# The first two units of a decoder block take the input without its norm factor, which is multiplied onto their results, and the order of the opening is written out

## The chip, the cores and the metric

The kernel runs on one core of one Trainium2 chip. The core has a matrix engine (TensorE, PE in the profile; PEld are its weight loads), VectorE (DVE), ScalarE (ACT), GpSimd (POOL) and a sync engine (SP), which here issues all the transfers between memory (HBM) and the on-chip buffer (SBUF). TensorE writes its results to PSUM, eight banks of 128 x 512 words. Each engine works through its own list of instructions in order and waits on semaphores for the others. The metric is the device time of one execution in microseconds (us).

## The reference, cut to what matters

One decoder block with 2048 positions and 1024 features, all in 32-bit floats. What the change touches is the first norm and the first part of the input projection:

```python
def rmsnorm(x, g):
    y = x * lax.rsqrt(jnp.mean(x * x, axis=-1, keepdims=True) + 1e-6)
    return y * g
...
h = rmsnorm(x, norm1_g)                      # one factor for each position, one gain for each feature
proj = h @ w_in                              # 1024 -> 3088 columns
p_q, p_k, p_v, p_g, p_a, c_b, c_c, c_h = jnp.split(proj, splits, axis=-1)
gate_logits = p_a @ w_gate_up + b_gate       # p_a has 16 columns
log_a = jax.nn.log_sigmoid(gate_logits) / 16
o = rmsnorm(gla_chunked(q, k, v, log_a), gla_norm_g) * jax.nn.silu(p_g)
o_conv = c_b * causal_depthwise_conv(c_c * c_h, conv_w)
x = x + concatenate([o, o_conv]) @ w_out
x = x + (silu(rmsnorm(x) @ w_ffn_gate) * (rmsnorm(x) @ w_ffn_up)) @ w_ffn_down
return rmsnorm(x, norm_f_g)
```

The norm multiplies every position by a number of its own (the norm factor) and every feature by a gain. Since a product with `w_in` sums over features, the factor of a position may be multiplied before the product or after it; the gain may not.

## The kernel before, in words

Data lie by features: a tile holds 128 features by 512 positions. There are four blocks of 512 positions; blocks 0 and 1 form half 0, blocks 2 and 3 half 1. The input comes twice: `x` by rows of positions and `xt` by features.

*Products.* A 32-bit product is made of three products in a shorter format (`fp32r`): every operand is split into a high part, a copy by ScalarE (L163), and a low part, a subtraction by VectorE (L164); the products are high x high, high x low and low x high (L448 to L450). `wq` names split weights and `op` split inputs.

*Units.* The input projection has 12 units for each half. A unit takes 256 output columns, 1024 input features and the 1024 positions of the half, each side as 2 x 2 quarters. Units 0 and 1 of half 0 are computed plainly, with 96 products (L362 to L364, and L448 to L450 from `plain_unit`). All others use seven quarter products of 12 instead of eight, so 84 products: `unit_weights` (L424 to L441) has GpSimd make the sums S1 to S4 of weight quarters (L430, L431, L432, L437), and the inputs are B11, B21, B22 and the differences T1 to T4. In half 0 the differences are made by VectorE (L374), each 4 tiles. The results of a unit's products are put together by ScalarE copies (L480) and VectorE additions (L473).

*Opening.* `first_loads` loads the four row tiles of block 0 in halves, then the weights of unit 0, the rows of block 1 and block 1 by features. Each half row tile is squared and summed by ScalarE (L595) and turned by TensorE to the layout by features (L600, into PSUM). `rows_rstd` makes the norm factor from the sums: Ln and Exp on ScalarE, a refinement step on VectorE (last line L177), copies of the factor to 128 x 128 tiles (`rep`, L552), which TensorE transposes (L555, `rb_ps`) so that the factor stands along positions. `build_first` then multiplies input, gain and factor (L615), splits the result and issues unit 0's products; the factor of block 1 is made in their midst. The order of the work here comes from a scheduler, steered by marks: `tc.issue_after(m)` puts an instruction behind another in time, without a wait in the program where they are on one engine.

*Background.* `tick()`, called after each group of 12 products, advances a list of side tasks by one step: the weights of the gate, `pause(8)`, the gate of half 0 with its forget gates (`forget_gate`; Abs, Exp and Ln on ScalarE, scans on VectorE, last line L745) in turn with the sums of squares of blocks 2 and 3 (`row_stats`), then `h1_ahead`. That one loads half 1's input (L145), multiplies it with its factor, makes its differences on GpSimd, splits and stores the operands (L148, names beginning with `si`) until half 1 loads them. ScalarE changes its table of functions between Exp or Ln and Silu; each change is an ACT_TABLE_LOAD.

*After that.* Units 4 and 5 give the columns of `silu` (L512), units 6 to 11 those of the convolution, whose first line is L784 and second L786. Then follow the attention in chunks (as further background; products at L869), half 1's units, the output projection (L945) and the feed-forward part. Nothing of these is changed.

Of the kernel before, what the change touches and what calls it, by code (L numbers as in the profile page):

```python
# [52 lines left out]
def tile_hymba_block(ctx, tc, x, xt, win, wa, wgu, wout, wffn, wdown, wdown_first, small, out):  # L53
# [98 lines left out]
    second_weights, unit_splits, unsplit = [], [], []  # L152
# [8 lines left out]

    def split(src, hi, lo):
        last_hi[:] = [act.activation(hi, src, AF.Copy)]  # L163
        last_lo[:] = [dve.tensor_tensor(lo, src, hi.bitcast(F32), ALU.subtract)]  # L164
        return last_lo[0]
# [156 lines left out]
    def build_first(quad, w):  # L322


        ops = {b: [] for _, b in PRODUCTS}
        h, o = {}, {}
        quarters = ("A11", "A12"), ("A21", "A22")
        los = []

        def weight(n, i, *marks):  # L330
            with ExitStack() as stack:
                for m in (last_exp[0], *marks):
                    stack.enter_context(tc.issue_after(m.ins))
                w[n] = weight_quarter(first_raw[0][:, i, :])

        weight("A11", 0, last_copy[0])
        los.append(last_lo[0])
        for j in range(2):
            for r in range(2):
                o[r, j] = bank()  # L340
            for k in range(KD):
                with tc.issue_after(los[-2 if len(los) > 2 else -1].ins):
                    h[k, j] = quad(k, j)
                if (j, k) == (0, 0):
                    weight("A21", 3, last_scaled[0])
                x = opp.tile([P, 2, PB], F32R, name="op", tag="op")
                los.append(split(h[k, j][:], x[:, 0, :], x[:, 1, :]))
                hi = last_hi[0]
                if j == 0 and k in (1, 2):
                    weight(*(("A12", 1), ("A22", 2))[k - 1], los[-1])  # L350
                if j == 0 and k < PT:
                    with tc.issue_after(hi.ins):
                        row_squares(k)
                if (j, k) == (0, PT + 2):
                    rbs[1] = rows_rstd(squares[1][:, :, 0])
                name = ("B11", "B12")[j] if k < 4 else ("B21", "B22")[j]
                ops.setdefault(name, []).append(x)
# [206 lines left out]
    def row_squares(t):  # L564
        act.activation(rows[t], rows[t], AF.Square, accum_out=squares[1][:, t, 0:1])
# [822 lines left out]
```

## Time and profile before

| | |
|---|---|
| time, median of 3 runs | 2060.74 us (2060.27 to 2066.71) |
| span of the profiled execution | 2059.3 us |
| instructions in it | 27063 |
| granted clock of TensorE over the span | 0.996 of full |
| memory read, written | 274.98 MB, 144.70 MB |

The page gives no other time for the profiled execution than its span, from the first to the last instruction. Engines overlap, so their busy times add up to far more than the span. The page lists busy time by engine, the span in 40 slices, the chain of work that ended last, and the costliest groups of instructions. A group's row has line, engine, operation, `output<-inputs` and count, then busy time and mean, then idle time ahead of it and what ended most of it. A row in order of time has the start in us, the duration in us, engine, line and tiles; in brackets stands the wait ahead of it and what ended it. `fp32r` is the shorter format of the products.

### The profile page before, as it was taken

Reading aid. Unit: us, or ns where it says so; the run is one execution under the profiler, and the core shown is the slowest. Engines: PE = TensorE matmul, PEld = TensorE weight load, DVE = VectorE, ACT = ScalarE, POOL = GpSimd, SP = SyncE. Lnnn points to the kernel's source line nnn. Section 1 sums busy time; section 2 is a strip of 40 time slices with the busy share of each in tenths; the row PEclk is TensorE's granted clock in tenths of the full one; section 3 lists DMA queues with packets and bytes.
Section 4 is the critical chain, followed back from the end, with each engine's and each line's share of the span. In section 5 each row is a group of like instructions: output and inputs, shape, how many; then the busy total and the mean of one; then the engine's idle time right before and its main releaser. Section 6 shows DMA issues by size and latency. Waiting matters only on the chain.

```text
span 2059.3 us, 27063 instructions
## 1 busy us (share of the span) xinstructions
PE 2018.4 (98%) x9229; PEld 1657.3 (80%) x9229; DVE 1425.3 (69%) x2128; ACT 959.7 (47%) x1918; POOL 859.8 (42%) x622
## 2 busy tenths in 40 slices
PE   7999999999999999999999999999999999999997
PEld 6877888787888888888888878787888888878786
DVE  8789686559743886676675676767666666667774
ACT  6655365765542344444444452334434444453344
POOL 0345322122102564464564345534644544435544
PEclk9999999999999999999999999999999999999998
DMA  6378485416586873545454676476444434586653
GB/s 229 116 274 278 159 319 165 143 67 194 190 296 246 311 254 130 198 181 207 156 185 143 241 264 254 185 282 257 163 164 167 175 140 169 179 309 223 234 217 126
DMA packets 188729, 421.47 MB, mean 205 GB/s; under 512 B 19792, under 2 KB 65072, under 8 KB 178992
## 3 DMA queue, kind: packets, MB, share of 16 engines
q1 hardware_dynamic: 188592, 419.76, 57.2%
q8 instruction: 72, 1.18, 0.2%
q14 instruction: 65, 0.53, 0.1%
HBM read 274.98 MB, written 144.70 MB: 204 GB/s over the span
## 4 chain that ended last, share of the span: by engine, by line
PE 84%; DVE 7%; DMA 4%; ACT 3%; issue 1%; POOL 1%; SPq 0%; DVEq 0%; ACTq 0%; POOLq 0%
PE mm L448 24%; PE mm L449 23%; PE mm L450 23%; PE mm L945 3%; PE mm L948 3%; PE mm L946 3%; DVE wq L164 2%; DVE op L164 1%; DMA op<-sa_B 1%; DMA op<-sa_T 1%; PE a_ps L702 1%; ACT wq L163 1%; DMA siT<-lo 1%; PE o_ps L869 1%; PE o_ps L871 1%
## 5 line engine op out<-in xcount | busy, mean ns | idle before, releaser
L448 PE MATMUL mm<-op,wq 128*128 128x512 f32 x2499 | 973.7, 392 | 10.3 <-ACT c L480 5.3
L449 PE MATMUL mm<-op,wq 128*128 128x512 f32 x2499 | 972.5, 390 | 1.6 <-DVE op L164 1.6
L450 PE MATMUL mm<-op,wq 128*128 128x512 f32 x2499 | 961.3, 390 | 2.6 <-DVE wq L164 2.3
L164 DVE TENSOR_TENSOR wq<-raw,wq 128x512 fp32r<-128x512 f32 (+2 forms) x626 | 508.9, 818 | 262.6 <-ACT wq L163 260.0
L163 ACT ACTIVATE wq<-raw 128x512 fp32r<-128x512 f32 (+2 forms) x626 | 364.9, 589 | 585.6 <-PE mm L450 447.9
L448 PEld LDWEIGHTS mm<-op,wq 128*128 128x128 f32 x2499 | 468.9, 188 | 114.9 <-ACT c L480 8.0
L450 PEld LDWEIGHTS mm<-op,wq 128*128 128x128 f32 x2499 | 469.1, 188 | 103.8 <-DVE wq L164 6.1
L449 PEld LDWEIGHTS mm<-op,wq 128*128 128x128 f32 x2499 | 469.3, 188 | 99.1 <-DVE op L164 3.7
L432 POOL TENSOR_TENSOR raw<-s,raw 128x512 f32<-128x512 f32 (+2 forms) x97 | 133.3, 1374 | 518.5 <-DVE wq L164 474.7
L430 POOL TENSOR_TENSOR s<-raw 128x512 f32<-128x512 f32 (+2 forms) x97 | 127.4, 1313 | 247.5 <-DMA raw<-in_wffn_dram 90.7
L473 DVE TENSOR_TENSOR c<-mm,c 128x512 f32<-128x512 f32 x198 | 135.8, 686 | 72.7 <-PE mm L450 70.9
L473 DVE TENSOR_TENSOR y<-mm,y 128x512 f32<-128x512 f32 x185 | 126.9, 687 | 83.3 <-PE mm L450 82.9
L437 POOL TENSOR_TENSOR raw<-raw 128x512 f32<-128x512 f32 (+2 forms) x97 | 120.6, 1244 | 126.7 <-DVE wq L164 126.7
L927 POOL TENSOR_TENSOR ssx<-ssx,q 128x512 f32<-128x512 f32 x52 | 77.4, 1504 | 158.8 <-ACT q L926 158.5
L431 POOL TENSOR_TENSOR raw<-raw 128x512 f32<-128x512 f32 (+2 forms) x97 | 137.3, 1416 | 4.9
L480 ACT ACTIVATE c<-mm 128x512 f32<-128x512 f32 x198 | 116.1, 587 | 11.1 <-PE mm L450 9.3
L945 PE MATMUL mm<-op,wq 128*128 128x512 f32 x256 | 100.9, 395 | 0.0
L946 PE MATMUL mm<-op,wq 128*128 128x512 f32 x256 | 99.7, 389 | 0.0
L163 ACT ACTIVATE wq<-s 128x512 fp32r<-128x512 f32 (+2 forms) x97 | 56.9, 587 | 89.3 <-PE mm L450 85.4
L164 DVE TENSOR_TENSOR wq<-s,wq 128x512 fp32r<-128x512 f32 (+2 forms) x97 | 82.6, 852 | 2.8 <-ACT wq L163 2.1
L164 DVE TENSOR_TENSOR op<-op 128x512 fp32r<-128x512 f32 x94 | 76.8, 844 | 4.7 <-ACT op L163 4.6
L948 PE MATMUL mm<-op,wq 128*128 128x512 f32 x256 | 79.8, 390 | 0.0
(204 smaller groups left out, 1807.6 us busy)
## 6 DMA issues: line engine op xcount, KB each, us to landing
raw<-in_wffn_dram SPq DMA_DIRECT2D x44, 1024.0 KB, 6.5
sa_B<-so SPq DMA_DIRECT2D x47, 512.0 KB, 4.2
op<-sa_B SPq DMA_DIRECT2D x47, 512.0 KB, 7.1
raw<-in_win_dram SPq DMA_DIRECT2D x23, 1024.0 KB, 5.4
sa_T<-so SPq DMA_DIRECT2D x44, 512.0 KB, 4.5
op<-sa_T SPq DMA_DIRECT2D x44, 512.0 KB, 6.9
raw<-in_wdown_dram SPq DMA_DIRECT2D x24, 768.0 KB, 5.8
sx<-y SPq DMA_DIRECT2D x48, 256.0 KB, 4.0
```

Source lines behind the costliest of these rows:

```text
L163: last_hi[:] = [act.activation(hi, src, AF.Copy)]
L164: last_lo[:] = [dve.tensor_tensor(lo, src, hi.bitcast(F32), ALU.subtract)]
L430: pool.tensor_tensor(s1, a21, a22, ALU.add)
L431: pool.tensor_tensor(a21, a11, a21, ALU.subtract)
L432: pool.tensor_tensor(a11, s1, a11, ALU.subtract)
L448: pe.matmul(o[:], wh, xh, start=first and k == 0, stop=False, skip_group_check=True)
L449: pe.matmul(o[:], wh, xl, start=False, stop=False, skip_group_check=True)
L450: return pe.matmul(o[:], wl, xh, start=False, stop=k == n - 1, skip_group_check=True)
L473: dve.tensor_tensor(t[:], o[:], t[:], ALU.add)
L945: pe.matmul(o[e, j][:], wh, m[:, 0, :], start=k == 0, stop=False)
L946: pe.matmul(o[e, j][:], wh, m[:, 1, :], start=False, stop=False)
L948: pe.matmul(o[e, j][:], wl, ops[k][j][:, 0, :], start=False, stop=k == KD - 1)
```

## The change

- *Units 0 and 1 of half 0* take the input of blocks 0 and 1 by features (`xt`) with the gain but without the norm factor. The gain is applied in the split (`split_in_order`): as the scale of ScalarE's copy and as the scalar of VectorE's operation. The factor is multiplied onto the 8 result tiles by VectorE (`out`), in place of ScalarE's copies.
- *Units from 2 on* take normed inputs as before. These are made by `normed` (input x gain x factor, 16 of them), and B11, B21 and B22, which before were the operands of units 0 and 1, are split once more (`made`).
- *The rows* of blocks 0 and 1 are still loaded and squared, for the factor; they are no longer turned by TensorE. Twelve products of a tile of ones (`warm`) are issued ahead of everything.
- *The order.* `opening` gives the order of loads, and `queued` puts each instruction of ScalarE and VectorE behind the one issued before on its engine. The low half of a split is issued behind the next split's high half (`late`, `catch_up`). Transposes of the factor are put behind a product in TensorE's order (`turn`): the first behind the first three steps of unit 0's second column, the second behind the first 24 products of unit 1. The products after them are put behind the transposes.
- *Unit 2* has the making of the last operands and the outputs of unit 1 put between the splits of its weights (`between`).
- *Background.* Unit 1 no longer calls `tick`. The list begins with `pause(1)`, the gate's weights, `pause(5)`.
- `rows_rstd`, now for blocks 2 and 3 alone, is what it was for them.

```diff
+    tails, late, ordered = {}, [], []
+    def queued(eng, issue):
+        with behind([tails[eng]] if eng in tails else []):
+            tails[eng] = issue()
+        return tails[eng]
+    def catch_up():
+        while late:
+            last_lo[:] = [queued(dve, late.pop(0))]
+    def split_in_order(src, hi, lo, gain=None):
+        scale = 1.0 if gain is None else gain
+        last_hi[:] = [queued(act, lambda: act.activation(hi, src, AF.Copy, scale=scale))]
+        catch_up()
+        top = hi.bitcast(F32)
+        if gain is None:
+            late.append(lambda: dve.tensor_tensor(lo, src, top, ALU.subtract))
+        else:
+            late.append(
+                lambda: dve.scalar_tensor_tensor(lo, src, gain, top, ALU.mult, ALU.subtract)
+            )
...
         w["S1"] = weight_quarter(s1)
+        others()
         w["S2"] = weight_quarter(a11)
+        others()
...
+        warm = bank("warm")
+        for _ in range(12):
+            pe.matmul(warm[:, 0:P], ones[:], ones[:], start=True, stop=True)
+        fetch_w(0)
+        fetch_x(0, 0)
+        fetch_w(3)
+        for k in (1, 2, 3):
+            fetch_x(k, 0)
+        fetch_w(1)
+        fetch_x(4, 0)
+        fetch_w(2)
+        fetch_x(5, 0)
+        for t in (0, 1):
+            fetch_rows(0, t)
+        for k in (6, 7):
+            fetch_x(k, 0)
+        for t in (2, 3):
+            fetch_rows(0, t)
+        for k in range(KD):
+            fetch_x(k, 1)
+        raw = raw_weights(win[1])
+        for t in range(PT):
+            fetch_rows(1, t)
+        raw2 = raw_weights(win[2])
...
+        def turn(rep, mark):
+            rb = bank("rb_ps")
+            with behind([mark]):
+                for t in range(PT):
+                    done = pe.transpose(rb[:, t * P : (t + 1) * P], rep[:, t, :], ident[:])
+            return rb, done
...
+        def normed(k, j):
+            y = h[k, j][:]
+            queued(
+                dve,
+                lambda: dve.scalar_tensor_tensor(
+                    y, y, col(C_G1 + k), rbs[j][:], ALU.mult, ALU.mult
+                ),
+            )
+        def out(o, dst, j):
+            c = tt("c")
+            queued(dve, lambda: dve.tensor_tensor(c[:], o[:], rbs[j][:], ALU.mult))
+            store(dst[:], c[:])
...
+        for k in range(KD):
+            column(k, 0)
+        operand(0, 1)
+        est = first_estimate(0)
+        operand(1, 1)
+        operand(2, 1)
+        rep = spread(*est)
+        catch_up()
+        for k in range(3):
+            mark = column(k, 1)
+        rb, turned = turn(rep, mark)
+        operand(3, 1)
+        keep(0, rb)
...
+        catch_up()
+        with behind([turned]):
+            for k in range(3, KD):
+                column(k, 1)
+        normed(2, 0)
+        out(o[0, 0, 0], s_kq[0][0], 0)
+        normed(3, 0)
+        out(o[0, 1, 0], s_kq[0][1], 0)
+        for n, i in (("A11", 0), ("A21", 3)):
+            weight(n, raw[:, i, :])
+        made("B11")
+        square(1, 0)
+        square(1, 1)
+        for n, i in (("A12", 1), ("A22", 2)):
+            weight(n, raw[:, i, :])
+        square(1, 2)
+        square(1, 3)
+        for k in range(4, KD):
+            normed(k, 0)
+        est = first_estimate(1)
+        catch_up()
+        rep = spread(*est)
...
+        rb, turned = turn(rep, second(0, 0))
+        keep(1, rb)
+        with behind([turned]):
+            for j, i in ((0, 1), (1, 0), (1, 1)):
+                second(j, i)
+        for k in range(4):
+            normed(k, 1)
+        for r in range(2):
+            out(o[0, r, 1], s_kq[1][r], 1)
+        for k in range(4, KD):
+            normed(k, 1)
+        made("T1")
+        between = [
+            [partial(made, "T2")],
+            [partial(out, o[1, r, 0], s_kq[0][2 + r], 0) for r in range(2)],
+            [partial(made, "B21")],
+            [partial(out, o[1, r, 1], s_kq[1][2 + r], 1) for r in range(2)]
+            + [partial(made, "T3")],
+            [partial(made, "B22")],
+            [partial(made, "T4")],
+        ]
+        return ops, raw2, between
...
-            gate_weights(), pause(8), in_turn(gate(0, ops), row_stats(2), row_stats(3)),
+            pause(1), gate_weights(), pause(5), in_turn(gate(0, ops), row_stats(2), row_stats(3)),
```

More of the change, by code (lines that the diff above doesn't have):

```diff
@@ L1250, in tile_hymba_block @@
     act.preload_act_table_set("natural_log_exp_and_others")
[L1251 to L1254 removed]
+    ops, raw, between = opening()
     hurry.append(True)
```

328 lines of the change are left out of this document (166 added, 162 removed).

## The prediction, made before the changed kernel had run

> **What bounds the kernel now.** I read the page first, then stretches of the span, then the order of time on single engines.
>
> ```profile
> span 2059.3 us, 27063 instructions
> PE 2018.4 (98%) x9229; PEld 1657.3 (80%) x9229; DVE 1425.3 (69%) x2128; ACT 959.7 (47%) x1918; POOL 859.8 (42%) x622
> PE   7999999999999999999999999999999999999997
> PE 84%; DVE 7%; DMA 4%; ACT 3%; issue 1%; POOL 1%; SPq 0%; DVEq 0%; ACTq 0%; POOLq 0%
> ```
>
> TensorE carries the chain; only the first and the last slice of 51 us show much idle time. The change touches the opening, so what counts is how late TensorE stands when unit 2, 3 and the later units of half 0 begin.
>
> ```profile
> core 0: us, PE busy (x) PEld busy (x) DVE busy (x) ACT busy (x) POOL busy (x), PEclk, DMA share, GB/s
> 0.00:16.39 16.39, 6.63 (x37) 5.77 (x37) 7.53 (x23) 10.47 (x26) 1.11 (x7) 1.00 0.84 294
> 16.39:63.82 47.43, 45.95 (x196) 37.61 (x197) 44.18 (x79) 27.86 (x54) 12.54 (x4) 0.96 0.48 176
> 63.82:83.10 19.28, 19.28 (x85) 15.76 (x84) 9.63 (x13) 10.46 (x22) 3.43 (x3) 1.00 0.27 95
> 120.00:145.00 25.00, 25.00 (x113) 20.61 (x112) 19.27 (x40) 14.23 (x25) 11.30 (x9) 1.00 0.73 250
> 145.00:200.00 55.00, 51.72 (x224) 41.50 (x223) 50.09 (x57) 25.84 (x49) 36.24 (x24) 1.00 0.89 305
> 10.00:20.00 10.00, 5.59 (x25) 4.33 (x24) 8.14 (x20) 8.35 (x21) 0.00 (x0) 0.83 1.04 403
> ```
>
> Rows are stretches (start:end, length), then busy time and count by engine. Units 0 and 1 (192 products of 512 columns, and 4 transposes) run from 16.39 to 63.82, unit 2 (84) to 83.10. In unit 2 TensorE issues 85 instructions in 19.28 us, 0.227 each, which is its full pace. So before 16.39 the time is lost, and VectorE is the next engine: 44.18 busy of 47.43, with slack only in unit 2 (9.63 of 19.28).
>
> ```profile
> 2.18 5.07 DMA xr<-in_x_dram
> 4.96 0.63 ACT L595 ACTIVATE q<-xr 128x512 f32<-128x512 f32 x1 [2.89 <-DMA xr<-in_x_dram]
> 16.39 0.73 PE L362 MATMUL mm<-op,wq 128*128 128x512 f32 x1 [2.42 <-ACT op L163]
> 19.90 0.39 PE L362 MATMUL mm<-op,wq 128*128 128x512 f32 x1
> 27.95 0.64 PE L555 MATMUL rb_ps<-ident,rep 128*128 128x128 f32 x4 [1.48 <-DVE rep L552]
> ```
>
> The first load is used at 4.96; the first product starts at 16.39, after transposes, norm factor and scaling. Up to 19.90 it runs at half clock (8 products in 3.51 us instead of 1.8: 1.7 lost), and block 1's factor costs 1.48 waited and 0.64 of transposes. With 1.7 and 2.1 lost, 192 x 0.227 = 43.6 becomes 47.4.
>
> **The change, step by step.**
>
> *Step 1, the start.* Gone: 32 transposes, 4 copies out of PSUM, the factor ahead of everything. The first product needs the second load of 256 KB (0.65 us each at 403 GB/s), so 4.96 + 0.65, and ScalarE's copy with a gain.
>
> ```profile
> L784 ACT ACTIVATE c<-u,sml 128x512 f32<-128x512 f32 x8 | 5.7, 718 | 4.1 <-DVE u L780 4.1
> 276.50 0.89 PE o_ps L869 x8
> ```
>
> The copy with a column as scale took 0.72, so the first product is at about 6.4. The 12 added warm-up products are plain fp32 (two records each): 0.11 a record as in the o_ps row, 0.22 a product, 0.44 at half clock, 5.3 us from 1.1 on, done at 6.4 as well. I take 6.5: **-9.9**. Whether the clock is full by then (0 or 1.7 lost) matters little, since the splits set the pace of the first products.
>
> *Step 2, the rest of units 0 and 1.* Loads are in the order of use, with 8 in flight. Counted in 256 KB, block 0's x(6) is the 15th (lands at 5 + 14 x 0.65 = 14), block 1's x(0) the 21st (18) behind four row tiles that ScalarE squares first. TensorE would want them at 15.5 and 18.7; with ScalarE's copies queued between, I count 3.0 us of waits on data in all, and 1.2 for the first weights of unit 1, whose low halves stand behind four products of the factor on VectorE. The larger wait is the second factor: its transposes stand in TensorE's order after 120 products, and 72 products are held behind them. They wait for VectorE, whose order is now given. Its built order up to the last `rep` holds 24 scalar_tensor_tensor, 14 tensor_tensor, 8 small operations and 8 copies.
>
> ```profile
> 28.63 1.41 DVE L615 SCALAR_TENSOR_TENSOR h<-h,sml,rb_ps 128x512 f32<-128x512 f32 x2 [0.42 <-PE rb_ps L555]
> 41.09 4.90 DVE L374 TENSOR_TENSOR h<-h 128x512 f32<-128x512 f32 x8
> 12.95 0.63 DVE L552 COPY rep<-msq 128x128 f32<-128x128 f32 x4
> 12.75 0.16 DVE L177 SCALAR_TENSOR_TENSOR msq<-rl,ry 128x4 f32<-128x4 f32 x1
> ```
>
> Back to back these are 0.66, 0.60, 0.18 and 0.2 apart: 15.8 + 8.4 + 1.6 + 1.4 = 27.2, from 5.5 on 32.7. It idles about 8 us on data and on ScalarE (3 for x(6), 2.7 for the squares and block 1's x(0), 1.6 for a copy that stands behind the factor's evacuation, the rest in short waits), and two GpSimd operations on unit 2's weights hold it 1.3 each (next rows). So `rep` is ready near 43.3. TensorE comes there at 6.5 + 120 x 0.227 + 3.0 + 1.2 + 0.5 = 38.4: a wait of 4.9. Unit 1 ends at 6.5 + 43.6 + 3.0 + 1.2 + 4.9 + 1.0 (two sets of transposes) = 60.2 against 63.82: **-3.6**.
>
> *Step 3, unit 2.* Twelve operands that were reused (B11, B21, B22) are now split anew from normed values: 12 more operations on each of ScalarE and VectorE; 16 normings replace 16 scalings; 8 results are multiplied by the factor on VectorE where ScalarE copied them.
>
> ```profile
> 54.12 8.83 POOL L432 TENSOR_TENSOR raw<-s,raw 128x512 f32<-128x512 f32 x1 [20.35 <-DVE wq L164]
> 61.12 0.69 DVE L374 TENSOR_TENSOR h<-h 128x512 f32<-128x512 f32 x1
> 62.99 0.64 ACT L163 ACTIVATE wq<-raw 128x512 fp32r<-128x512 f32 x1 [3.76 <-POOL raw L432]
> 106.33 1.63 POOL L432 TENSOR_TENSOR raw<-s,raw 128x512 f32<-128x512 f32 x1 [10.13 <-DVE wq L164]
> 106.70 1.28 DVE L216 TENSOR_TENSOR rl<-msq,ry 128x4 f32<-128x4 f32 x1
> ```
>
> VectorE and GpSimd exclude each other here: the GpSimd subtraction started at 54.12 ended only after VectorE's dense stream did (61.81, then 1.1 us), and at 106.70 a 0.16 us operation took 1.28 behind one. From `rep` to the last low half of T4 VectorE's order holds 8 scalar_tensor_tensor and 60 tensor_tensor: 5.3 + 36.0 = 41.3, from 44.6 (the factor is copied first) to 85.9; three GpSimd operations in the way at 1.3 and the copies' latencies add 4.6: 90.5. The first product on that operand is the 298th: without waits at 60.2 + 105 x 0.227 = 84.1. So **+6.4**, which leaves +2.8 at unit 3. Ends: 0, if VectorE keeps up, and 9, if the exclusion strikes each of the seven weights.
>
> *Step 4, the table loads.* The background list starts with unit 2 instead of unit 1: 8 calls fewer ahead of it and 2 less of pause, so 6 groups of 12 products, 16.3 us, later. The forget gates' Exp and Ln then fall beside unit 4's Silu.
>
> ```profile
> 111.90 0.21 ACT L745 ACTIVATE el<-g 128x4 f32<-128x4 f32 x1
> 120.88 1.28 ACT L512 ACT_TABLE_LOAD   x1
> 122.17 0.63 ACT L512 ACTIVATE c<-c 128x512 f32<-128x512 f32 x1
> ```
>
> Before, the last of them ended 9 us ahead of the first Silu. The built order holds 20 table loads against 15, the five extra ones around units 4 and 5: 5 x 1.28 = 6.4 us on an ACT that is busy 14.23 of 25 there. That share, 0.57, gives **+3.7**; ends 0 and 6.4. The Trainium skill (ScalarE: Activation LUTs, What ACT_TABLE_LOAD costs) gives 1283 ns and a drain of 1380 ns to every switch; the trace agrees with the first and shows 1.29 from the load to the next activation. By that page's 2.66 us the five would be 13.3, an estimate.
>
> *Step 5, what comes late after that.* Half 1's operands are made ahead in one chain of loads, VectorE, GpSimd and stores:
>
> ```profile
> 123.68 1.61 SPq L145 DMA_DIRECT2D h<-in_xt_dram  x3
> 188.11 1.78 DVE L786 SCALAR_TENSOR_TENSOR c<-u,sml,c 128x512 f32<-128x512 f32 x1
> 192.04 0.38 SPq L148 DMA_DIRECT2D siT<-t  x1
> ```
>
> It ran from 123.68 to 192.04, and TensorE lost 55.0 - 224 x 0.227 = 4.2 us from 145 to 200. It reached only 4 us into the convolution (first row of L786); some 20 us later it lies beside it and the loads of the attention stage, on a VectorE that was at 50.09 of 55 already. I take the loss once more: **+4.2**; ends 0 (it merely moves) and 8.4 (three times). The order from there on is the old one, and nothing gives time back.
>
> Sum: -3.6 + 6.4 + 3.7 + 4.2 = +10.7. That is 2070.0 against the profiled execution's 2059.3, which stands 1.4 under the median shown, so **2071 us**.
>
> **Rivals.**
> - *VectorE keeps up* (faster). If idle time on data in the opening goes and the factor is ready by 38.4, step 2 gives -8.5; it decides if T4 is then split by 79 instead of 90. The 8 us of idling speak for it, the sum of 27.2 + 41.3 against it: even dense it ends at 74 plus five holds of 1.3, 80. With steps 4 and 5 hidden: 2052.
> - *The later units absorb it.* ACT has room in 120 to 145, and the chain of step 5 has its own slack: only steps 1 to 3 count, +2.8: 2063.5. For it speaks TensorE's full 25.00 there.
> - *The switches cost more.* With the drain as a full stop of ACT on the path (5 x 2.66 for 3.7) and step 5 at its upper end: 2059.3 + 2.8 + 13.3 + 4.2 + 1.4 = 2081. The 1.29 speaks against it. By the page this is what would happen.
>
> **How the numbers follow.** 0.3% is 6.2 us, about what a measurement here can tell from none: 2054.6 to 2066.9 counts as the same. My forecast gets 0.57, VectorE keeping up 0.08, absorption 0.24, costly switches 0.11. The forecast's lower edge reaches into "same" rarely and absorption's upper edge out of it as often, so faster 0.08, same 0.24, slower 0.68. The range leaves out the faster case and the top of the costly one: 2061 (steps 4 and 5 nearly free) to 2080 (their upper ends, 6.4 and 8.4, are 2078).
>
> **What would show it.** Step 1: first product at 6 to 7 us. Step 2: a wait of TensorE on `rep` near 38, 3 to 7 us long. Step 3: TensorE waits on low halves of op in unit 2, between 62 and 92, 6 us in all, VectorE busy over 90% from 20 to 90. Step 4: 20 table loads, five of them within 120 to 145, and waits of TensorE on ACT there. Step 5: the last siT store near 215 and over 6 us lost between 145 and 225; from 300 on the same distance to the trace of before. The prediction is wrong if unit 2 ends before 80, or if the distance shrinks after 145.

## The result and the profile after

The changed kernel takes 2087.8 us (median of 4 runs, 2084.6 to 2088.6) against 2061.2: 26.6 us or 1.21% slower, ratio 1.0121 with a 95% interval of 1.0106 to 1.0135. The forecast was 2071 us. The direction came out as said, the size did not: by the end of half 0's convolution the trace is 24.75 us behind, where the prediction's sum was 10.7.

The page of the changed kernel: its first lines, VectorE's row of the 40 slices, and the chain.

```profile
span 2082.9 us, 27063 instructions
...
PE 2029.3 (97%) x9221; PEld 1658.5 (80%) x9221; DVE 1436.8 (69%) x2143; ACT 968.0 (46%) x1920; POOL 853.6 (41%) x622
...
DVE  7877777558764596766776577775775676677774
...
PE 80%; DVE 9%; DMA 5%; ACT 3%; issue 2%; POOL 0%; SPq 0%; DVEq 0%; ACTq 0%; POOLq 0%
```

The profiled execution is the fastest of the four (2084.6); its span is 23.6 us longer than before. VectorE's share of the chain rose from 7 to 9%, TensorE's fell from 84 to 80%.

To place the loss, count the long products of the units (512 columns, into `mm`) in the order in which they ran, and compare the start of the nth in both traces; the nth is here the one that has n ahead of it. The distance, after minus before, is -9.5 us at the first, -1.6 at the 192nd (end of unit 1), +10.0 at the 360th (as many as units 0 to 3 have; of the gate's 36 products the old kernel has done all by then and the changed one all but one), +17.6 at the 556th, and +24.75 from the 840th to beyond the 1000th. Below, stretches of the changed kernel cut at these products (start:end, length, then busy time and count by engine):

```profile
core 0: us, PE busy (x) PEld busy (x) DVE busy (x) ACT busy (x) POOL busy (x), PEclk, DMA share, GB/s
0.00:6.90 6.90, 5.49 (x25) 5.20 (x25) 2.33 (x8) 2.63 (x3) 1.11 (x7) 1.00 0.59 162
6.90:62.19 55.29, 48.61 (x201) 38.08 (x201) 45.59 (x76) 31.33 (x56) 7.29 (x5) 0.94 0.62 232
62.19:120.42 58.23, 51.74 (x205) 38.31 (x204) 43.52 (x65) 30.38 (x62) 11.14 (x8) 0.97 0.31 107
120.42:175.51 55.09, 47.32 (x206) 37.50 (x205) 42.69 (x97) 40.33 (x81) 19.76 (x14) 1.00 0.65 224
175.51:249.67 74.16, 67.55 (x282) 53.01 (x280) 61.63 (x81) 35.23 (x68) 36.86 (x25) 0.98 0.78 264
```

Before, the same stretches took 16.39, 47.43, 46.59, 47.48 and 67.03 us. So the start gained 9.5, and the four after it lost 7.9, 11.6, 7.6 and 7.1. The prediction had -9.9, then +6.3, +6.4, +3.7 and +4.2: every loss is there, and every one is too small.

Rows in order of time show the forecast wait on the second factor, and two of the waits in unit 2:

```profile
43.24 1.09 PE L630 MATMUL rb_ps<-ident,rep 128*128 128x128 f32 x4 [4.50 <-DVE rep L620]
...
69.62 0.50 PE L410 MATMUL mm<-op,wq 128*128 128x512 f32 x1 [1.59 <-DVE op L182]
...
95.91 0.50 PE L410 MATMUL mm<-op,wq 128*128 128x512 f32 x1 [1.33 <-DVE op L182]
```

What the prediction did not have is in the granted clock (column PEclk), shown here in stretches of 3.41 us, the steps in which it changed:

```profile
core 0: us, PE busy (x) PEld busy (x) DVE busy (x) ACT busy (x) POOL busy (x), PEclk, DMA share, GB/s
34.15:37.56 3.41, 3.41 (x17) 2.79 (x16) 3.41 (x6) 3.41 (x7) 0.53 (x1) 1.00 0.85 289
37.56:40.97 3.41, 1.18 (x6) 0.64 (x4) 3.41 (x4) 0.49 (x2) 2.84 (x2) 1.00 0.02 9
40.97:44.38 3.41, 1.14 (x5) 1.18 (x6) 2.42 (x11) 0.43 (x3) 0.00 (x0) 0.50 0.22 43
44.38:47.79 3.41, 3.41 (x9) 2.64 (x9) 2.80 (x5) 0.58 (x1) 0.00 (x0) 0.50 0.75 303
47.79:51.20 3.41, 3.41 (x16) 2.81 (x16) 3.41 (x6) 0.00 (x0) 0.00 (x0) 1.00 0.41 154
...
68.27:71.69 3.42, 1.34 (x5) 0.82 (x6) 3.42 (x5) 2.24 (x5) 1.67 (x1) 1.00 0.71 230
71.69:75.10 3.41, 3.41 (x10) 2.63 (x9) 3.41 (x7) 0.00 (x0) 0.00 (x0) 0.50 0.17 64
```

After a stretch in which TensorE was idle most of the time, the next is at half clock: 9 or 10 instructions in 3.41 us instead of 16. The wait of 4.5 us thus cost about 2.3 us more behind it (4.5 us of products at half speed), the waits around 70 about 1.7 (3.4 us at half speed); a third such stretch follows at 180.9.

### The profile page after: what moved, and what is told of

The parts are those of the page before. It is cut to its first block, busy times and chain, and to the rows that moved or that the text cites. A ratio compares the mean times of both kernels' runs of the same rounds, so it can differ in the third digit from the quotient of the medians.

```text
span 2082.9 us, 27063 instructions
## 1 busy us (share of the span) xinstructions
PE 2029.3 (97%) x9221; PEld 1658.5 (80%) x9221; DVE 1436.8 (69%) x2143; ACT 968.0 (46%) x1920; POOL 853.6 (41%) x622
## 4 chain that ended last, share of the span: by engine, by line
PE 80%; DVE 9%; DMA 5%; ACT 3%; issue 2%; POOL 0%; SPq 0%; DVEq 0%; ACTq 0%; POOLq 0%
PE mm L409 23%; PE mm L411 23%; PE mm L410 23%; PE mm L1093 2%; PE mm L1096 2%; PE mm L1094 2%; DVE wq L192 2%; DVE op L192 1%; DMA h<-in_xt_dram 1%; PE a_ps L856 1%; DMA ee<-sd 1%; ACT wq L191 1%; DVE op L182 1%; PE o_ps L1017 1%; PE o_ps L1019 1%
## 5 line engine op out<-in xcount | busy, mean ns | idle before, releaser
L409 PE MATMUL mm<-op,wq 128*128 128x512 f32 x2467 | 963.1, 393 | 17.6 <-ACT c L444 9.7
L410 PE MATMUL mm<-op,wq 128*128 128x512 f32 x2467 | 961.9, 390 | 6.0 <-DVE op L182 5.7
L411 PE MATMUL mm<-op,wq 128*128 128x512 f32 x2467 | 950.5, 391 | 5.0 <-DVE wq L192 4.9
L192 DVE TENSOR_TENSOR wq<-raw,wq 128x512 fp32r<-128x512 f32 (+2 forms) x612 | 494.8, 813 | 258.2 <-ACT wq L191 255.5
L191 ACT ACTIVATE wq<-raw 128x512 fp32r<-128x512 f32 (+2 forms) x612 | 355.6, 587 | 577.1 <-PE mm L411 440.3
L409 PEld LDWEIGHTS mm<-op,wq 128*128 128x128 f32 x2467 | 463.9, 188 | 123.8 <-ACT c L444 13.0
L411 PEld LDWEIGHTS mm<-op,wq 128*128 128x128 f32 x2467 | 463.7, 188 | 106.4 <-DVE wq L192 10.1
L410 PEld LDWEIGHTS mm<-op,wq 128*128 128x128 f32 x2467 | 464.0, 188 | 105.3 <-DVE op L182 9.7
L387 POOL TENSOR_TENSOR raw<-s,raw 128x512 f32<-128x512 f32 (+2 forms) x97 | 125.2, 1290 | 526.8 <-DVE wq L192 459.4
L1093 PE MATMUL mm<-op,wq 128*128 128x512 f32 x256 | 100.9, 395 | 0.0
L1094 PE MATMUL mm<-op,wq 128*128 128x512 f32 x256 | 99.7, 390 | 0.0
L1096 PE MATMUL mm<-op,wq 128*128 128x512 f32 x256 | 79.8, 390 | 0.0
```

Of the source, the lines that this page charges most:

```text
L387: pool.tensor_tensor(a11, s1, a11, ALU.subtract)
L409: pe.matmul(o[:], wh, xh, start=first and k == 0, stop=False, skip_group_check=True)
L410: pe.matmul(o[:], wh, xl, start=False, stop=False, skip_group_check=True)
L411: return pe.matmul(o[:], wl, xh, start=False, stop=k == n - 1, skip_group_check=True)
L1093: pe.matmul(o[e, j][:], wh, m[:, 0, :], start=k == 0, stop=False)
L1094: pe.matmul(o[e, j][:], wh, m[:, 1, :], start=False, stop=False)
```

## The experiments

Each kernel was run 4 to 11 times beside the old one on the same chip (the old one's median 2061.7 to 2062.9). "Faster" and "slower than the changed one" compare medians with its 2087.8; the interval of each ratio is 2 to 3 us to either side, so smaller differences between two runs are not shown by their times. Distances at the nth product are to the trace of the old kernel, as above.

### Is it the opening, or the background that it pushed back?

First run: the old kernel, with the background alone as late as in the changed one.

```diff
-            gate_weights(), pause(8), in_turn(gate(0, ops), row_stats(2), row_stats(3)),
+            gate_weights(), pause(14), in_turn(gate(0, ops), row_stats(2), row_stats(3)),
```

> The old kernel with its old opening, and only the background put where the changed kernel has it (6 product groups later; 20 table loads instead of 15). Theory A: the 14.8 us that the changed kernel loses between its 360th and its 840th product come from the late background alone; then this kernel is slower than before by 12 to 16 us, with the same distance of about 15 by the 840th product. Rival B: the background costs what the prediction priced (3.7 + 4.2 = 7.9), the rest comes from the opening, which leaves VectorE and ScalarE behind: slower by 6 to 9. Rival C: it is hidden when the opening is the old one: within 3 us.

Measured: 2073.7, ratio 1.0050 (1.0035 to 1.0064), so 11.4 us slower, and a distance of +0.2 at the 360th product and +12.7 at the 840th. That is just under A's 12 and far above the prediction's 7.9: of the 14.75 us that the changed kernel lost there, 12.5 come with the late background on the old opening too.

Second: the changed kernel with the background early.

```diff
-            pause(1), gate_weights(), pause(5), in_turn(gate(0, ops), row_stats(2), row_stats(3)),
+            gate_weights(), in_turn(gate(0, ops), row_stats(2), row_stats(3)),
```

> The changed kernel with both pauses of the background taken out, so that the gate's products stand after 264 of the long products instead of 300 and the program has 15 table loads. Theory A: the part after the 360th product falls from 14.8 us to 2 or less, and the kernel comes to 2070 to 2075; some of the gain is paid back in unit 2 and 3, where VectorE is full. Rival B: the loss stays above 6 us, as it is the opening's: 2078 to 2081. Rival C: the earlier background strikes the full VectorE in unit 2 and 3 and loses there what it saves: 2084 to 2088.

Measured: 2080.2, ratio 1.0088 (1.0072 to 1.0103). From the 360th to the 840th product only 1.5 us are lost, as A says. But at the 360th the distance is +16.2 instead of +10.0: between 61 and 115 us TensorE waits 6.4 us for high and low halves of unit 2's last operands, and runs at half clock for 10.2 and for 3.4 us. Both A and C are in it: 13.3 us saved late, 6.2 paid early. The time lies in B's range, but not by B's mechanism.

Fifth: the gate's steps first, the sums of squares after them, so that the forget gates end before the first Silu.

```diff
-            pause(1), gate_weights(), pause(5), in_turn(gate(0, ops), row_stats(2), row_stats(3)),
+            pause(1), gate_weights(), pause(4), gate(0, ops), row_stats(2), row_stats(3),
```

> The changed kernel with the second pause at 4 and the gate's steps ahead of the sums of squares instead of in turn with them: the forget gates end before the first Silu, the program has 15 table loads instead of 20, and the making of half 1's operands begins as late as before this edit. Theory (the table loads are the rise of 7.4 us between the 360th and the 500th product): this rise falls to 2 or less, the later one (7.2 us from the 556th to the 836th) stays, and the kernel is 5 to 7 us faster than the changed one: 2080 to 2083. Rival (the rise is ScalarE's whole load there, squares and splits, and not the loads of tables): within 2 us of it.

Measured: 2089.4, ratio 1.0127 (1.0112 to 1.0143): not faster. The rise went as the theory said: from the 360th to the 556th product 1.9 us instead of 7.6. But the distance at the 360th is +17.3, 7.3 more, probably since the gate's work now falls beside the operands of units 2 and 3 (not tested by itself), and the later rise is 9 instead of 7.1. So 5.8 us go with the five loads; the gate's own activations left the stretch with them, so that is their price together, while the squares of blocks 2 and 3 stayed there, so they alone don't make the loss. Moving the gate alone only moves the loss.

In the changed kernel, ScalarE's table loads in order of time:

```profile
132.93 1.28 ACT L476 ACT_TABLE_LOAD   x1
134.87 1.28 ACT L890 ACT_TABLE_LOAD   x1
140.88 1.28 ACT L897 ACT_TABLE_LOAD   x1
143.01 1.28 ACT L476 ACT_TABLE_LOAD   x1
145.57 1.28 ACT L899 ACT_TABLE_LOAD   x1
148.84 1.28 ACT L476 ACT_TABLE_LOAD   x1
```

and the stretch around them, from 120 to 145, where ScalarE was busy 14.23 us before:

```profile
core 0: us, PE busy (x) PEld busy (x) DVE busy (x) ACT busy (x) POOL busy (x), PEclk, DMA share, GB/s
120.00:145.00 25.00, 22.34 (x97) 17.84 (x96) 22.29 (x56) 23.14 (x51) 5.72 (x4) 1.00 0.65 230
```

Six where one stood, on a ScalarE that is now full: the squares of blocks 2 and 3 crowd there as well.

Sixth: the old kernel with only the making of half 1's operands late.

```diff
-            unhurried(),
+            pause(6), unhurried(),
```

> The old kernel with six more steps of pause between the sums of squares and the making of half 1's operands: forget gates and table loads (15) where they were, only that chain 6 product groups later. Theory (the chain beside the convolution costs by itself): slower than before by 5 to 8 us, the rise lying behind the 550th product. By the prediction's price it would be 4.2. Rival (it merely moves): within 2 us, and the 12.7 us of the first run were the table loads and what they delay.

Measured: 2069.7, ratio 1.0032 (1.0020 to 1.0045), slower by 7.3 us between the medians and by 6.6 by the ratio; the trace has +5.2 at the 840th product, all of it behind the 600th. The chain costs by itself when it is late.

Thirteenth: the same, with the chain's 16 differences on VectorE instead of GpSimd.

```diff
-    def combine(src, g, rb, put):
+    def combine(src, g, rb, put, eng=pool):
...
-            pool.tensor_tensor(t1[:], b12[:], b11[:], ALU.subtract)
+            eng.tensor_tensor(t1[:], b12[:], b11[:], ALU.subtract)
...
-        yield from combine(lambda k, j: xt[2 + j, :, k, :], C_G1, (rbs[2], rbs[3]), put)
+        yield from combine(lambda k, j: xt[2 + j, :, k, :], C_G1, (rbs[2], rbs[3]), put, dve)
...
```

> The sixth run (old kernel, half 1's operands made six product groups later, 6.6 us slower) with the 16 differences of that chain made by VectorE instead of GpSimd. Theory (what the late chain costs is GpSimd's holds on VectorE beside the convolution, as in unit 2): most of the 5.2 us that the trace lost there goes, 0 to 3 us slower than the old kernel. Rival (loads and the copies in ScalarE's queue set it, not GpSimd): 5 to 8 us slower as before this edit.

Measured: 2060.2, ratio 0.9996 (0.9987 to 1.0005): the 6.6 us are gone. The groups of VectorE between 157 and 230 us show what changed there. The sixth run (count, busy time, mean ns of one):

```profile
L164 DVE TENSOR_TENSOR lo<-t,hi 128x512 fp32r<-128x512 f32 x6 | 6.1, 1024 | 3.5 <-ACT hi L163 3.5
L164 DVE TENSOR_TENSOR lo<-h,hi 128x512 fp32r<-128x512 f32 x5 | 5.7, 1131 | 0.0
```

and the thirteenth:

```profile
L164 DVE TENSOR_TENSOR lo<-t,hi 128x512 fp32r<-128x512 f32 x6 | 4.1, 680 | 0.0
L164 DVE TENSOR_TENSOR lo<-h,hi 128x512 fp32r<-128x512 f32 x5 | 3.4, 681 | 0.0
```

Without GpSimd's differences the chain's own low halves take 0.68 us each instead of 1.02 and 1.13. The chain itself is shorter too: its last store of `siT` starts at 198.8 us instead of 204.1. How much each of the two is worth was not separated.

Fourteenth: this edit with the chain at its old time.

> The old kernel with the same edit alone (chain at its old time). Between 145 and 200 us TensorE lost 4.2 us. Theory: GpSimd's holds are part of that, 1 to 4 us faster than the old kernel. Rival: the same within 1 us.

Measured: 2063.7, ratio 1.0013 (1.0004 to 1.0022): no gain, 2 us slower if anything, which neither the theory nor the rival had. The trace is 5.4 us behind at the 800th product, most of it lost in one wait of 2.7 us on a ScalarE copy that ends at 203.5 us and a stretch of 6.8 us at half clock around it. That a chain without GpSimd is faster at any time is not shown; that it is no longer dear when late is.

### What bounds unit 2?

Third: the second factor's transposes behind 48 products of unit 1.

```diff
-        rb, turned = turn(rep, second(0, 0))
+        second(0, 0)
+        rb, turned = turn(rep, second(0, 1))
...
-            for j, i in ((0, 1), (1, 0), (1, 1)):
+            for j, i in ((1, 0), (1, 1)):
```

> The changed kernel with the transposes of the second factor put behind 48 products of unit 1 instead of 24, so that TensorE has 5.4 us of work while it waited 4.5 us for the factor (and ran at half clock for 6.8 us after). Theory (VectorE sets the pace to the end of unit 2): unit 1 ends about 6 us earlier, and nearly all of it goes back in unit 2, where the operands T2 to T4 come no earlier: the end changes by less than 2 us. Rival: the wait stands on the path: 5 to 7 us faster than the changed kernel, 2078 to 2082.

Measured: 2084.5, ratio 1.0104 (1.0089 to 1.0119), 3.3 us faster than the changed one. The trace says the same as the theory: unit 1 ends 3.8 to 5.3 us earlier (-5.4 at the 192nd product, -6.9 at the 180th), and at the 276th only 0.9 of it is left. TensorE's wait moved to unit 2. In time the run lies between the theory (less than 2) and the rival (5 to 7); at the 840th product the trace has 2.0.

Fourth: the outputs of units 0 and 1 copied by ScalarE, the factor left out.

```diff
-            queued(dve, lambda: dve.tensor_tensor(c[:], o[:], rbs[j][:], ALU.mult))
+            queued(act, lambda: act.activation(c[:], o[:], AF.Copy))
```

> The changed kernel with the 8 results of units 0 and 1 copied out by ScalarE without the factor, where VectorE multiplied them (the factor is left out of k and q): 8 x 0.6 = 4.8 us less on VectorE up to the end of unit 2. Theory (VectorE sets the pace there): TensorE starts unit 3 by 3 to 5 us earlier, and the kernel is 2 to 5 us faster than the changed one. Rival: unit 2 waits for latencies and for the hold by GpSimd, not for VectorE's amount of work: within 1 us.

Measured: 2080.8, ratio 1.0085 (1.0070 to 1.0099), 7.0 us faster, more than the theory's 2 to 5; the trace has 5.0 at the 840th product. The last low half of T4 starts at 90.9 us instead of 96.4, and at the 360th product the distance is 4.2 us smaller. So 4.8 us less work on VectorE brought the operands about as much earlier.

Seventh: no sums of weight quarters by GpSimd in units 2, 3 and 4.

```diff
+        sums = len(units_seen) > 3
...
-        pool.tensor_tensor(s1, a21, a22, ALU.add)
-        pool.tensor_tensor(a21, a11, a21, ALU.subtract)
-        pool.tensor_tensor(a11, s1, a11, ALU.subtract)
+        if sums:
+            pool.tensor_tensor(s1, a21, a22, ALU.add)
+            pool.tensor_tensor(a21, a11, a21, ALU.subtract)
+            pool.tensor_tensor(a11, s1, a11, ALU.subtract)
+        else:
+            s1 = a11
...
```

> The changed kernel without GpSimd's sums of weight quarters in units 2, 3 and 4 (single quarters are used in their place, so the results of these units are others; splits and products stay). Theory (GpSimd holds VectorE): nine sums from 37 to 95 us take 1.1 each from VectorE, so the last low half of T4 comes 8 to 10 us earlier than 97 us, the distance to the old kernel at the 360th product falls from +10.0 to between 2 and 5, and the kernel is 5 to 8 us faster than the changed one: 2080 to 2083. Rival (VectorE's amount of work and the order of the copies set it): T4 less than 3 us earlier and the kernel within 3 us.

Measured: 2073.0, ratio 1.0046 (1.0034 to 1.0059), 14.8 us faster, about twice what the theory gave. T4's last low half starts at 85.2 us, 11.2 earlier, and the distance at the 360th product is -1.4 instead of +10.0.

Ninth: the sums of these units on VectorE.

```diff
+NSUM = 3
...
+        by = dve if len(units_seen) <= NSUM else pool
...
-        pool.tensor_tensor(s1, a21, a22, ALU.add)
+        by.tensor_tensor(s1, a21, a22, ALU.add)
...
```

> The changed kernel with the sums of weight quarters of units 2, 3 and 4 made by VectorE instead of GpSimd. That gives VectorE 12 x 0.6 = 7.2 us more work and takes away up to nine holds of 1.1. Theory (GpSimd's sums cost more than their holds, since they also wait for a gap in VectorE's stream and weights wait for them; without them altogether the distance at the 360th product fell by 11.4): it falls by 3 to 6, and the kernel is 3 to 7 us faster than the changed one: 2081 to 2085. Rival (VectorE's amount of work decides): no gain or a loss, 2086 to 2092.

Measured: 2085.1, ratio 1.0104 (1.0087 to 1.0120). The time is at the edge of the theory's range, but not by its mechanism: unit 2's first sum was put ahead of low halves of the opening in VectorE's order, waited there for the load of its weights, and TensorE stood 9.1 us until 38.5. This run says nothing on the question, but something on queues: one early instruction that waits for a late load holds all behind it.

Eleventh: the same with the sums put behind what stands before them in VectorE's order.

```diff
+            if not own:
+                pool.tensor_tensor(y, a, b, op)
+            elif ordered:
+                queued(dve, lambda: dve.tensor_tensor(y, a, b, op))
+            else:
+                with behind([tails[dve]]):
+                    dve.tensor_tensor(y, a, b, op)
...
```

> The ninth run again (sums of units 2 to 4 on VectorE), with the sums put behind what stands before them in VectorE's order; there one of them had stood ahead of the opening's low halves and held TensorE 9.4 us for the load of unit 2's weights. Theory (GpSimd's sums cost TensorE more than their work does on VectorE): unit 1 ends as in the changed kernel or up to 3 us earlier, the distance at the 360th product falls from +10.0 to between 3 and 7, the kernel is 3 to 7 us faster than the changed one: 2081 to 2085. Rival (VectorE's amount of work): 2086 to 2091.

Measured: 2075.6, ratio 1.0059 (1.0045 to 1.0074), 12.2 us faster, with all sums still made, which is well above the theory's 3 to 7. At the 360th product the distance is +2.0 instead of +10.0. This settles the question: 12 more operations on VectorE are much cheaper here than 12 on GpSimd beside it. In the changed kernel, GpSimd's sums and VectorE's operations beside them, in order of time:

```profile
57.51 1.29 POOL L387 TENSOR_TENSOR raw<-s,raw 128x512 f32<-128x512 f32 x1 [17.04 <-DVE wq L182]
59.48 1.62 POOL L385 TENSOR_TENSOR s<-raw 128x512 f32<-128x512 f32 x1 [0.68 <-POOL raw L387]
61.19 1.62 POOL L386 TENSOR_TENSOR raw<-raw 128x512 f32<-128x512 f32 x1
...
57.67 1.68 DVE L182 TENSOR_TENSOR wq<-s,wq 128x512 fp32r<-128x512 f32 x1 [0.30 <-ACT wq L178]
59.27 2.38 DVE L652 TENSOR_TENSOR h<-h 128x512 f32<-128x512 f32 x2
61.58 1.78 DVE L182 TENSOR_TENSOR op<-h,op 128x512 fp32r<-128x512 f32 x1
63.29 0.68 DVE L652 TENSOR_TENSOR h<-h 128x512 f32<-128x512 f32 x1
```

Three sums, three VectorE operations that take 1.0 to 1.1 us longer than the 0.68 of the one that follows. From the factor to T4 the changed kernel's VectorE:

```profile
core 0: us, PE busy (x) PEld busy (x) DVE busy (x) ACT busy (x) POOL busy (x), PEclk, DMA share, GB/s
44.00:97.00 53.00, 47.24 (x180) 34.96 (x178) 48.94 (x69) 23.14 (x43) 11.27 (x8) 0.93 0.26 95
```

and the eleventh run's:

```profile
core 0: us, PE busy (x) PEld busy (x) DVE busy (x) ACT busy (x) POOL busy (x), PEclk, DMA share, GB/s
44.00:86.00 42.00, 37.80 (x156) 28.40 (x155) 41.20 (x68) 20.45 (x38) 0.00 (x0) 1.00 0.29 103
```

Nearly as many instructions (69 and 68) in 48.94 and in 41.20 us: 7.7 us, with eight sums of GpSimd in that stretch. Seven of them (57.51 to 93.09) lengthen seven VectorE operations, six by 1.0 to 1.1 us and one by 0.5, 7.0 together. The other 3.3 of the 11 us are idle time (4.06 us against 0.80). Most of it is one wait, which the eleventh run does not have:

```profile
77.84 0.69 DVE L437 TENSOR_TENSOR c<-mm,c 128x512 f32<-128x512 f32 x1 [2.38 <-ACT op L178]
...
96.38 0.68 DVE L182 TENSOR_TENSOR op<-h,op 128x512 fp32r<-128x512 f32 x1
```

The first row adds up results of unit 2 and stands in VectorE's order ahead of the operands still to be made; the last of the products that it adds starts at 77.36, after TensorE's own waits for low halves and the half clock from 71.69. So the two engines hold each other up in turn. The second row is T4's last low half.

### The start

Eighth: one product of ones instead of twelve.

```diff
-        for _ in range(12):
-            pe.matmul(warm[:, 0:P], ones[:], ones[:], start=True, stop=True)
+        pe.matmul(warm[:, 0:P], ones[:], ones[:], start=True, stop=True)
```

> The changed kernel with one of the twelve products of ones ahead of everything. Theory: the clock stays at half until some 3 to 7 us after the first product, but the splits of the first operands set the pace, so the 36th product comes no more than 1 us later and the end is the same within 2 us. Rival: the products of ones are worth 2 to 4 us.

Measured: 2086.7, ratio 1.0115 (1.0101 to 1.0129), no difference from the changed one. The clock is at half until 10.8 us instead of 6.8, the 36th product comes 0.9 us later, the 48th at the same time.

### Put together

Tenth: turn later, the factor of units 0 and 1 multiplied onto k and q in the attention, the sums of units 2 to 4 on VectorE, second pause at 3.

```diff
...
+            load(e[:, 0, :], s_rb[b][:, s])
+            dve.tensor_tensor(kq[:], kq[:], e[:, 0:1, :].to_broadcast([P, 4, P]), ALU.mult)
...
-            pause(1), gate_weights(), pause(5), in_turn(gate(0, ops), row_stats(2), row_stats(3)),
+            pause(1), gate_weights(), pause(3), in_turn(gate(0, ops), row_stats(2), row_stats(3)),
```

> What the runs point to, put together: the second factor's transposes behind 48 products (3.3 us gained before), the outputs of units 0 and 1 stored without the factor, which is stored too and multiplied onto k and q when the attention loads them (7 us gained by leaving it out, against 8 x 0.6 on VectorE later), the sums of units 2 to 4 on VectorE (3 to 6 expected), and the second pause at 3, so that the program has one table load fewer than the old kernel. If the gains add up: 2062 to 2070. Rival (VectorE is still full in units 2 and 3, and the earlier gate pays there what the table loads save, as in the fifth run): 2072 to 2080. Faster than the old kernel only if the late chain of operands costs nothing as well.

Measured: 2085.6, ratio 1.0110 (1.0095 to 1.0125); the ninth run's early sum is in it, with a wait of 9.7 us. Twelfth, with the sums in place:

> The tenth run again with the sums in the same places as in the eleventh. The gains one by one: 3.3 (turn later), 7 (outputs without the factor), 3 to 7 (sums), and from the earlier gate what the table loads save less what unit 3 pays for it, -3 to +5. If they add: 2066 to 2075. Rival (each of them frees the same VectorE time, so that they don't add): 2075 to 2081. It beats the old kernel in neither case.

Measured: 2072.9, ratio 1.0050 (1.0037 to 1.0062). Against the eleventh run's 2075.6 the three other gains (3.3, 7.0 and the table loads) bring 2.7 together: they don't add. The time lies in the theory's range all the same, but only because the sums alone gave 12.2 where 3 to 7 were reckoned.

Fifteenth: the fourteenth run's kernel with the sums of units 3 to 11 of half 0 on VectorE.

```diff
+NSUM = 10
...
+        eng = dve if 1 < len(units_seen) <= NSUM else pool
...
-        pool.tensor_tensor(s1, a21, a22, ALU.add)
+        eng.tensor_tensor(s1, a21, a22, ALU.add)
...
```

> The fourteenth run's kernel with the sums of weight quarters of units 3 to 11 of half 0 on VectorE too. Theory: where VectorE has room nothing changes, and beside the convolution it saves the rest: 2 to 5 us faster than the old kernel. Rival: VectorE, at 50 of 55 us there, gets too much work: slower by 1 to 5.

Measured: 2059.4, ratio 0.9989 (0.9980 to 0.9998): the fastest of all, 2.3 us (0.1%) below the old kernel, at the lower edge of the theory; that is less than the 0.3% that counts as a change here. In the trace TensorE lost 1.7 us between 145 and 200 (55.0 - 235 x 0.227) where it was 4.2.

Sixteenth: the twelfth run's kernel with the chain's differences on VectorE.

> The twelfth run's kernel (unit 2's sums on VectorE, turn later, outputs without the factor, earlier gate; 2072.9) with the differences of the late chain on VectorE. It lost 10 us between the 584th and the 880th product. Theory (GpSimd's holds): 4 to 8 us of them go, 2065 to 2069. Rival: within 2 us of 2073.

Measured: 2066.2, ratio 1.0029 (1.0017 to 1.0040), 6.7 us faster than the twelfth, as the theory says. Seventeenth, the sums of all units of half 0 on VectorE, and eighteenth, T1 made earlier and the second pause at 2:

```diff
+        made("T1")
         for r in range(2):
             out(o[0, r, 1], s_kq[1][r], 1)
         for k in range(4, KD):
             normed(k, 1)
-        made("T1")
...
```

> The sixteenth run's kernel (2066.2) with the sums of units 5 to 11 of half 0 on VectorE too, which was worth 4 us between the fourteenth and the fifteenth run. If the same holds here: 2061 to 2064. Rival: VectorE, later here by the gate's work, has no room beside the convolution: 2066 to 2070.

> The same with T1 made before the last four normed inputs of block 1 and the second pause at 2. TensorE waited 4.5 us in unit 2 for the low half of T2, which this does not bring earlier; T1 comes 2.6 us earlier, so that S1 x T1 need not wait. Theory: 0 to 2 us faster than the run before it. Faster than the old kernel (2061.7) only if both edits hold.

Measured: 2069.9, ratio 1.0034 (1.0022 to 1.0046), and 2068.1, ratio 1.0027 (1.0017 to 1.0038). The seventeenth lands in its rival's range (2066 to 2070); the eighteenth is 1.8 us faster than it, as its theory has it. All three are the same within their intervals and 0.3% slower than the old kernel: they start 9.4 to 9.5 us earlier, are 9.0 to 9.3 ahead at the 192nd product, and 3.4 to 5.4 behind at the 360th. With GpSimd out of the way, the changed opening still gives back in units 2 and 3 all that it gained: VectorE is busy 55.7 of 65.5 us from 54.5 to 120 in the sixteenth run, and TensorE waits 4.3 us at once for ScalarE's high half of a difference that VectorE makes late.

## Why the prediction was right and wrong

The losses came in the places that were named, but all four were forecast too small. Of the 14.05 us between the sum (+10.7) and the trace's 24.75, step 1 has 0.4, step 2 1.6, step 3 5.2, step 4 3.9 and step 5 2.9. The step that failed most is the third: it took three holds of VectorE by GpSimd where seven came, and put at nothing both the half clock behind TensorE's waits and the wait of VectorE on a late TensorE. Steps 4 and 5 together, the late background, were priced at 7.9 and cost 14.75. And the range left out that the upper ends come together.

*Step 1, the start (-9.9).* Right: the first product at 6.90 us, -9.5. That the clock would not matter there was right too (eighth run).

*Step 2, rest of units 0 and 1 (+6.3).* Right in its wait, wrong in the size: +7.9. The wait on the second factor is 4.50 (4.9 forecast; it begins at 38.7, forecast 38.4). The term that was missing is the clock behind it: the prediction reckoned with half clock at the start alone, and here it came again behind a wait, for 2.3 us.

*Step 3, unit 2 (+6.4).* Right in the mechanism, mis-sized: with unit 3 +11.6. The list of 8 and 60 operations stood as counted. But GpSimd's sums held VectorE seven times instead of three up to T4's last low half (57.51 to 93.09), 7.0 us in all where three holds were reckoned at 1.3, 3.9. The upper end of 9 us was to hold for the seven weights of unit 2, but four more holds at 1.3 make 6.4 + 5.2 = 11.6. Seven came, and from sums of units 2, 3 and 4 (two, three and two), which are made at the same time; that the sum then meets the measured 11.6 is luck, since the holds were shorter and the rest is waits. VectorE's wait of 2.38 us ahead of 77.84 and about 1.7 us of half clock came on top. T4's last low half, forecast to be done at 90.5, is done at 97.1. One reading behind the step was wrong, though its sum does not hang on it: the stretch from 63.82 to 83.10 in the old trace is not unit 2's 84 products but 52 long products and the gate's 32, and the 84th long product after unit 1 starts at 90.7. The Trainium skill (SBUF — State Buffer, SBUF: two separate sides) has the rule: a VectorE operation with two inputs in SBUF and a GpSimd operation that reads SBUF lock a port pair against each other, for the whole instruction. The rows above agree, with 1.0 to 1.1 us for each sum but one.

*Step 4, table loads (+3.7).* Right in the cause as far as shown, mis-sized in the share: +7.6 to the 556th product, of which 5.8 go when the five loads and the gate's activations beside them do. 5 x 1.28 = 6.4 was the upper end. The share of 0.57 was ScalarE's busy time in the old trace; in the changed kernel ScalarE is busy 23.14 of 25 us there, since the squares come late with the gate. The other 1.8 us were not traced to a cause. The share should have been taken from what the late background does to that stretch.

*Step 5, the late chain (+4.2).* Right in place, low in size: +7.1 in the changed kernel, and 7.3 alone on the old opening (6.6 by the ratio). The last store of `siT` starts at 224.2, forecast near 215. The loss was put to loads and a full VectorE. On the old opening it is gone when VectorE makes the 16 differences instead of GpSimd, so GpSimd's part in it is shown, by its holds on VectorE or by the longer chain. 1.7 us of it is again half clock, at 180.9.

*The rivals.* "VectorE keeps up" fell with step 3. "The later units absorb it" fell most clearly: the first run shows 11.4 us for the late background alone. "The switches cost more" comes nearest in its total, by luck and not by its mechanism: from a table load to the next activation it is still 1.29 us (132.93 to 134.22), and the five cost at most 5.8, not 13.3. Its sum was also added up wrong: with step 5 at its upper end of 8.4, as its words say, it gives 2059.3 + 2.8 + 13.3 + 8.4 + 1.4 = 2085.2 and not 2081. The measured time lies above all four cases; all took each shared resource at its price for one stage. The sum of upper ends (9 instead of 6.4, 6.4 instead of 3.7, 8.4 instead of 4.2: 20.2, or 22.8 with 11.6 for the first) is near the 24.75; the range left them out together as too unlikely. That they came together fits one common cause, a VectorE without slack; for steps 3 and 5 the runs support it, for the table loads on ScalarE it is not shown.

## What to carry to other kernels

When an edit fills an engine that was next to the bound, price every later step at its upper end: the slack that made the middle value likely is what the edit used up. An idle engine is no free help if its work holds up the full one: 12 sums moved from GpSimd to VectorE, the busier engine, made the changed kernel 12 us faster. And a shorter opening is worth only what the next full engine lets through; look for the stage whose list of work decides when the operands are there, and count it from the same start.

## What the runs showed of the hardware that was not expected

The granted clock falls to half after a short wait, without a long pause. The traces of these 20 kernels, cut in steps of 3.41 us on the clock's own grid, show it up to 2030 us, ahead of the kernels' ends: all 44 steps at full clock in which TensorE was idle 2.0 us or more were followed by a step at half clock, none of about 11,700 with less than 1.5 us idle were, and 8 of 59 in between. The Trainium skill (TensorE: Matmul & The Clock Gate, What's actually happening) has the step of about 3.4 us and the two states, but puts the fall behind at least one idle step; here a step with 1.34 us of work in 3.42 (68.27 to 71.69) was enough. So the waits of 1.59 and 0.73 us, which lie mostly in that step, cost nearly as much again: 10 products of 512 columns instead of 16 in the next 3.41 us, about 1.7 us.
